# A two-layer hybrid block on one Trainium2 core: the order of its instructions set by the framework's timeline simulator instead of its simpler model

## The chip, the core and the metric

The kernel runs on one core of a Trainium2 chip. A core has a matrix engine (TensorE, PE in the rows; its weight loads are PEld), a vector engine (DVE), a scalar engine (ACT), GpSimd (POOL) and SyncE (SP), which issues the transfers here. Each engine works through its own list of instructions in the order in which it was written, and waits on semaphores where an instruction needs what another engine makes. The metric is the device time of one execution in microseconds.

## The reference, cut to what matters

Two layers work on 256 latent tokens and 256 context tokens of width 1024. The last layer needs the latent tokens alone behind its first FFN (in its mixers the context is read only).

```python
for l in range(2):
    mod = silu(c) @ ada_w[l] + ada_b[l]        # nine vectors: shift, scale, gate, three times
    x  = x + 0.5 * g1 * swiglu(modulate(rms_norm(x), sh1, sc1))          # FFN, 2816 wide
    u  = modulate(rms_norm(x), sh2, sc2)
    o_a = attention(u)     # MLA, 8 heads
    o_b = gla(u)           # gated linear attention, 4 heads, both directions, chunks of 64
    o_c = attention(u)     # GQA, 8 heads
    o_d = hyena(u)         # two long convolutions by DFT
    y   = sum(sigmoid(gate_i(u)) * (o_i @ w_branch[i]) for i in 4) @ w_out
    x  = x + g2 * y
    x  = x + 0.5 * g3 * swiglu(modulate(rms_norm(x), sh3, sc3))
```

## The kernel before

Everything is float32. A product is made of three matmuls on split operands: each operand is cut into a rounded part and the rest (`two`, L309: ACT writes `wh` at L311, DVE writes `wl` at L312, in one stage of layer 1 sometimes POOL), and `mm3` (L303) issues high by high, high by low and low by high, all at L301. Weights arrive by transfers into `wr` (three buffers) and leave the split into `wh` and `wl` (eight each).

The stages run one behind another: adaLN vectors (`ada`, L413, sixteen short matmuls with the weights of a vector from memory), statistics and norm (L487 and L513, tiles `sq`, `nacc`, `st`, `rs`, `B`, then `uh` and `ul`), the FFN (`gu`, `dn`), the mixers, the merges, `wo`, the FFN again. The mixers are chains: in the gated linear attention (GLA) a head goes from `pre` (PE) over the forget gates (ACT L992 to L994, DVE L995, L996), two scans (L998, L1000), exponentials (L1009 to L1013), products (L1014 to L1016), `AT` (PE), masks (L1026, L1030), `keT`, `ke`, `U` and the states (L1051, L1053: seven small DVE steps for each direction, one behind another) to `Og` (PE), its norm (`z`, L1065 to L1071) and `obT` (PE). Attention goes from `S` (PE) over maximum, exponential, sum, reciprocal and product (L684 to L688) to `PT` and `O` (PE). Hyena goes back and forth between spectra (`Z`, `yi` on PE) and products on ACT and DVE (`Yh`, `Yl`).

`weave` (L1326) puts beside such chains, the fill, work that waits for nothing but weights: in layer 0 the projections of `prep` (`tm`, `bk`, `bq`) beside hyena, then the merge of one finished branch (`gate`, `br`, `mt`, `y`) beside each next mixer; in layer 1 `prep` beside both attentions, and two merges beside hyena and GLA together:

```python
for c in list(chains):
    with self.first():                  # tc.high_priority(offset=200)
        if next(c, 0) is not None:
            chains.remove(c)
more = next(fill, 0) is None
```

The order on each engine isn't the order of the code. The framework takes the whole program, with priorities from the place in the code, raised by 200 in the chains (`first`) and by 400 in `evac` (L296), and hands out the instructions of each engine one by one: at each step the one that its model of time holds to be ready, the higher priority first. The model therefore decides how much fill stands between two links of a chain. Before, that is the framework's simpler model.

## Time and profile before

| | |
|---|---|
| median of three runs | 2607.05 us (2606.05 to 2609.52) |
| the profiled execution | 2601.85 us, span 2600.1 us |
| granted clock of PE, mean | 0.986 of full |
| busy: PE, DVE, ACT, POOL | 2497.5, 1696.6, 1091.1, 264.9 us |

PE is the engine that bounds; the rest of this document asks where it stands still and for whom. The rows further down tell a stretch of the span by its start and end in microseconds. A matmul's own duration overlaps that of its neighbours, so the time of dense work is read from the length of a stretch over its count.

### The profile page before, as it was taken

The page shows a single profiled execution, that of the slowest core. Times are in us where ns is not written, and L with a number is a line of the kernel's source. Part 1 is how long each engine was busy: PE and PEld are TensorE (multiplying, and loading weights), DVE is VectorE, ACT ScalarE, POOL GpSimd, SP SyncE. Part 2 cuts the span into 40 slices and gives each one's busy share as a digit, 9 for nine tenths or more (in the row PEclk, how much of TensorE's full clock was granted, in tenths as well). Part 3 has the DMA queues.
Part 4 walks back from the last instruction along what each step waited for, and adds up shares of the span by engine and source line. Part 5 has one row for each costly group of instructions (what it writes and reads, how often), then busy time and mean ns, then how long its engine had stood idle before and what let it go on. Part 6 is the DMA issues. An engine that isn't in the chain of part 4 may idle for free. (4 is left out here: it accounts for less than half of the span.)

```text
span 2600.1 us, 36866 instructions
## 1 busy us (share of the span) xinstructions
PE 2497.5 (96%) x13624; PEld 2058.8 (79%) x13624; DVE 1696.6 (65%) x3377; ACT 1091.1 (42%) x2127; POOL 264.9 (10%) x240
## 2 busy tenths in 40 slices
PE   6999999999999999999999999999999987899998
PEld 4778887887877667777888878888888777788998
DVE  5667858577547778746744466767458667776665
ACT  4333223333545554433232343232346664455554
POOL 2110003001000000020000030000020147401000
PEclk9999999999999999999999999999999999899999
DMA  7564535332313123245623244545353333356554
GB/s 253 176 213 170 190 128 192 134 108 100 126 57 122 61 88 106 89 156 174 205 97 97 86 158 146 178 146 174 102 187 130 114 120 122 114 161 210 177 184 124
DMA packets 122371, 369.01 MB, mean 142 GB/s; under 512 B 14090, under 2 KB 19660, under 8 KB 122192
## 3 DMA queue, kind: packets, MB, share of 16 engines
q1 hardware_dynamic: 122192, 366.66, 42.8%
q8 instruction: 107, 1.75, 0.3%
q14 instruction: 72, 0.59, 0.1%
HBM read 346.16 MB, written 20.45 MB: 141 GB/s over the span
## 5 line engine op out<-in xcount | busy, mean ns | idle before, releaser
L311 ACT CAST wh<-wr 128x512 fp32r<-128x512 f32 (+1 forms) x926 | 564.0, 613 | 1070.3 <-PE gu L301 396.0
L312 DVE TENSOR_TENSOR wl<-wr,wh 128x512 fp32r<-128x512 f32 (+1 forms) x854 | 577.1, 682 | 410.1 <-ACT wh L311 399.3
L301 PE MATMUL gu<-ul,wh 128*128 128x512 f32 (+1 forms) x1408 | 514.7, 366 | 2.5 <-DVE ul L542 2.5
L301 PE MATMUL gu<-uh,wh 128*128 128x512 f32 (+1 forms) x1408 | 512.3, 366 | 2.4 <-ACT uh L536 2.3
L301 PE MATMUL gu<-uh,wl 128*128 128x512 f32 (+1 forms) x1408 | 511.5, 364 | 1.3 <-DVE wl L312 1.3
L301 PE MATMUL dn<-hh,wh 128*128 128x512 f32 (+1 forms) x1408 | 389.5, 363 | 0.0
L301 PEld LDWEIGHTS gu<-ul,wh 128*128 128x128 f32 x1408 | 265.7, 189 | 58.4 <-DVE ul L542 9.3
L301 PEld LDWEIGHTS gu<-uh,wh 128*128 128x128 f32 x1408 | 265.8, 189 | 52.0 <-ACT uh L536 7.2
L301 PEld LDWEIGHTS gu<-uh,wl 128*128 128x128 f32 x1408 | 265.6, 189 | 44.0 <-DVE wl L312 1.7
L301 PEld LDWEIGHTS dn<-hh,wh 128*128 128x128 f32 x1408 | 252.6, 188 | 41.3
L301 PE MATMUL dn<-hh,wl 128*128 128x512 f32 (+1 forms) x704 | 255.3, 363 | 0.0
L502 POOL TENSOR_TENSOR nacc<-nacc,sq 128x512 f32<-128x512 f32 (+1 forms) x39 | 46.2, 1185 | 1745.1 <-ACT sq L500 1736.7
L301 PE MATMUL gate<-uh,wh 128*128 128x256 f32 (+1 forms) x768 | 202.3, 328 | 3.3 <-DVE y L1316 3.3
L464 DVE SCALAR_TENSOR_TENSOR aj<-aw,crow 128x1024 bf16<-128x1024 f32 x160 | 193.7, 1224 | 0.0
L301 PE MATMUL gate<-uh,wl 128*128 128x512 f32 (+1 forms) x512 | 177.0, 346 | 4.3 <-POOL wl L312 2.8
L301 PEld LDWEIGHTS dn<-hh,wl 128*128 128x128 f32 x704 | 132.3, 188 | 20.4
L301 PEld LDWEIGHTS gate<-uh,wh 128*128 128x128 f32 x768 | 132.0, 195 | 15.4 <-DVE y L1316 3.5
L301 PE MATMUL tm<-wh,uh 128*128 128x256 f32 x576 | 140.3, 288 | 1.6 <-ACT uh L536 1.0
L312 POOL TENSOR_TENSOR wl<-wr,wh 128x512 fp32r<-128x512 f32 x72 | 106.4, 1489 | 239.9 <-ACT wh L311 234.1
L301 PE MATMUL tm<-wl,uh 128*128 128x256 f32 x432 | 124.1, 287 | 0.0
L301 PEld LDWEIGHTS gate<-uh,wl 128*128 128x128 f32 x512 | 99.1, 194 | 15.9 <-POOL wl L312 3.0
L642 DVE SCALAR_TENSOR_TENSOR x<-dn,gt,x 128x256 f32<-128x256 f32 x168 | 74.4, 478 | 54.6 <-PE dn L301 54.6
(408 smaller groups left out, 3975.7 us busy)
## 6 DMA issues: line engine op xcount, KB each, us to landing
wr<-in_gu SPq DMA_DIRECT2D x176, 512.0 KB, 3.5
aw<-in_adat SPq DMA_DIRECT2D x80, 512.0 KB, 3.6
wr<-in_dn SPq DMA_DIRECT2D x64, 512.0 KB, 3.6
wr<-in_w_gate SPq DMA_DIRECT2D x64, 512.0 KB, 3.5
aw<-in_ada SPq DMA_DIRECT2D x48, 512.0 KB, 4.6
wr<-in_w_tm SPq DMA_DIRECT2D x36, 512.0 KB, 3.6
wr<-in_w_br SPq DMA_DIRECT2D x32, 512.0 KB, 3.5
wr<-in_dn SPq DMA_DIRECT2D x32, 384.0 KB, 3.2
```

Source lines behind the costliest of these rows:

```text
L301: self.nc.tensor.matmul(out, l, r, start=start, stop=stop)
L311: self.nc.scalar.copy(h, src)
L312: (eng or self.nc.vector).tensor_sub(l, src, h)
L464: nc.vector.scalar_tensor_tensor(out=x, in0=w, scalar=1.0, in1=self.crow[s], op0=ALU.mult, op1=ALU.mult, accum_out=o[:, s:s + 1])
L502: (nc.vector if first and k % 2 else nc.gpsimd).tensor_add(acc[:, :n], acc[:, :n], sq[:, :n])
L642: self.nc.vector.scalar_tensor_tensor(out=self.x[m][:, c], in0=p[:, c], scalar=gt[:, m, s:s + 1], in1=self.x[m][:, c], op0=ALU.mult, op1=A ...
```

## The change

One argument is added where the framework's context is made:

```diff
-    with tile.TileContext(nc, ) as tc:
+    with tile.TileContext(nc, schedule_with_timeline_sim=True) as tc:
         emit(tc, A, out)
```

No instruction is added or taken away (one of ACT's nineteen loads of a function table stands at another place); each engine's list is put in another order. PE's list changes most: most of the rows that differ lie in the woven stages. POOL's list stays almost as it was. Three places follow, all on PE; numbers behind a name are those of the buffers, the same before and after.

**Layer 0, GLA, second to third head.** `Og_9482` is the product that ends the second head, `AT_9670` the first matmul of the third behind its forget gates, `gate` and `br` are the merge. Before:

```order
L301 MATMUL Og_9482<-STl_9412,qd_9290 64x128 x2
L301 MATMUL Og_9482<-bv_8917,ATs_9393 128x128
L301 MATMUL Og_9482<-STl_9412,qd_9290 64x128 x2
L301 MATMUL Og_9482<-bv_8919,ATs_9393 128x128
L301 MATMUL Og_9482<-STc_9413,qd_9290 64x128 x2
L301 MATMUL Og_9482<-bv_8919,ATs_9393 128x128
L301 MATMUL Og_9482<-STc_9413,qd_9290 64x128 x2
L301 MATMUL gate_9537<-uh_3745,wl_9541 128x512
L301 MATMUL gate_9537<-uh_3755,wh_9544 128x512
L301 MATMUL gate_9537<-ul_3756,wh_9544 128x512
```

After:

```order
L301 MATMUL Og_9482<-STl_9412,qd_9290 64x128 x2
L301 MATMUL Og_9482<-bv_8919,ATs_9393 128x128
L301 MATMUL Og_9482<-STc_9413,qd_9290 64x128 x2
L301 MATMUL Og_9482<-bv_8919,ATs_9393 128x128
L301 MATMUL Og_9482<-STc_9413,qd_9290 64x128 x2
L301 MATMUL AT_9670<-qd_9589,ab_9597 128x128
L301 MATMUL AT_9671<-qd_9589,ab_9597 128x128
```

What moved: before, 37 `gate` and 17 `br` matmuls stand between `Og_9482` and `AT_9670`; after, none. From `AT_9381` to `obT_9878`, the last of the head behind, 36 matmuls of fill are left after (12 `gate`, 24 `br`), and the other ones stand further ahead, beside the first head and its setup. The same holds in layer 1 for the third of the GLA heads, and for the later heads of the attentions, between whose links a few `br` stand or nothing.

**Layer 0, hyena, from the first spectra to `yi`.** `tm` and `bk` are projections of `prep`. Before:

```order
L301 MATMUL tm_5177<-wh_5331,uh_3775 128x256
L301 MATMUL tm_5177<-wl_5332,uh_3775 128x256
L301 MATMUL tm_5177<-wh_5331,ul_3776 128x256
L301 MATMUL tm_5177<-wh_5331,uh_3785 128x256
L301 MATMUL tm_5177<-wl_5332,uh_3785 128x256
L301 MATMUL tm_5177<-wh_5331,ul_3786 128x256
L301 MATMUL yi_5649<-Yh_5595,dfth_4277 128x512
L301 MATMUL tm_5178<-wh_5181,uh_3715 128x256
L301 MATMUL tm_5178<-wl_5182,uh_3715 128x256
```

After:

```order
L301 MATMUL bk_5537<-ul_3776,wh_5544 128x512
L301 MATMUL bk_5537<-uh_3775,wl_5545 128x512
L301 MATMUL bk_5537<-uh_3785,wh_5544 128x512
L301 MATMUL bk_5537<-ul_3786,wh_5544 128x512
L301 MATMUL bk_5537<-uh_3785,wl_5545 128x512
L301 MATMUL bq_5611<-uh_3715,wh_5614 128x512
L301 MATMUL bq_5611<-ul_3716,wh_5614 128x512
L301 MATMUL yi_5649<-Yh_5595,dfth_4277 128x512
L301 MATMUL bq_5611<-uh_3715,wl_5615 128x512
L301 MATMUL bq_5611<-uh_3725,wh_5614 128x512
L301 MATMUL bq_5611<-ul_3726,wh_5614 128x512
L301 MATMUL bq_5611<-uh_3725,wl_5615 128x512
```

What moved: before, the fill from the last `Z` (`Z_5528`) to `yi_5649` is 73 `tm` matmuls of 256 columns; after, 42 `tm` and 50 `bk` and `bq`, these of 512 columns. The `bk` and `bq` stood beside later work.

**The norm between layer 0's second FFN and layer 1's first.** `st` sums the squares, `B` spreads the factors, `ada_13691` is the next adaLN vector, `dn` the FFN's end, `gu` the start of the next FFN. Before:

```order
L301 MATMUL st_13561<-ones_104,nacc_13560 128x1 x4
L301 MATMUL ada_13691<-aw_13692,cs_106 32x512 x2
L301 MATMUL ada_13691<-aw_13696,cs_106 32x512 x2
L301 MATMUL ada_13691<-aw_13700,cs_106 32x512
L301 MATMUL st_13561<-ones_104,sq_13581 128x1 x4
L301 MATMUL ada_13691<-aw_13700,cs_106 32x512
L301 MATMUL ada_13691<-aw_13704,cs_106 32x512 x2
L301 MATMUL ada_13691<-aw_13708,cs_106 32x512 x2
L348 MATMUL B_13606<-ident_100,rs_13591 128x128 x4
L301 MATMUL ada_13691<-aw_13712,cs_106 32x512 x2
L301 MATMUL ada_13691<-aw_13716,cs_106 32x512 x2
L301 MATMUL gu_13746<-uh_13614,wh_13738 128x512
```

After:

```order
L301 MATMUL dn_13537<-hh_13306,wl_13534 128x512
L301 MATMUL ada_13691<-aw_13712,cs_106 32x512 x2
L301 MATMUL ada_13691<-aw_13716,cs_106 32x512 x2
L301 MATMUL ada_13691<-aw_13720,cs_106 32x512 x2
L301 MATMUL st_13561<-ones_104,nacc_13560 128x1 x4
L301 MATMUL st_13561<-ones_104,sq_13581 128x1 x4
L348 MATMUL B_13606<-ident_100,rs_13591 128x128 x4
L301 MATMUL gu_13746<-uh_13614,wh_13738 128x512
L301 MATMUL gu_13781<-uh_13614,wh_13773 128x512
```

What moved: the fourteen `ada` matmuls that stood between `st` and `gu`, and two behind the first `gu`, are gone from there; six stand ahead of `st`, and the other ten over a thousand rows further up, among the FFN's matmuls. The norm behind the first FFN of layer 1 shows the same, and at the one behind the first FFN of layer 0 all sixteen moved up.

## Rows read from the trace of the kernel before

**Rows 1.** The page: busy time and share of the span of each engine
```profile
PE 2497.5 (96%) x13624; PEld 2058.8 (79%) x13624; DVE 1696.6 (65%) x3377; ACT 1091.1 (42%) x2127; POOL 264.9 (10%) x240
```

**Rows 2.** Stretches: length, busy PE, PEld, DVE, ACT, POOL (x instructions), clock, DMA share, GB/s
```profile
1180.00:1528.00 348.00, 348.00 (x1537) 288.24 (x1536) 183.72 (x325) 108.91 (x182) 7.72 (x6) 1.00 0.39 128
...
840.00:945.00 105.00, 104.47 (x512) 71.31 (x511) 73.41 (x192) 59.22 (x158) 0.00 (x0) 1.00 0.20 62
...
992.40:1076.00 83.60, 79.63 (x442) 59.74 (x441) 66.02 (x154) 33.90 (x56) 0.00 (x0) 1.00 0.32 101
...
2178.40:2233.60 55.20, 37.65 (x237) 31.92 (x236) 45.39 (x76) 21.76 (x42) 28.81 (x17) 0.85 0.31 100
```

**Rows 3.** PE's waits by releaser: total us, times, longest us
```profile
PE st L301 <- POOL nacc L502: 14.9, 2, 14.0
...
PE AT L301 <- DVE ab L1015: 10.4, 5, 4.3
...
PE obT L348 <- DVE z L1071: 7.5, 5, 3.3
...
PE yi L301 <- ACT Yh L311: 6.5, 4, 2.7
...
PE aT L348 <- ACT ck L761: 3.5, 1, 3.5
```

**Rows 4.** Groups of PE, two of 992.4 to 1076, one of 2178.4 to 2233.6: busy, mean ns
```profile
L301 PE MATMUL gate<-ul,wh 128*128 128x512 f32 x62 | 24.7, 399 | 0.0
...
L301 PE MATMUL br<-oc,wh 128*128 128x512 f32 x24 | 7.7, 402 | 0.0
...
L301 PE MATMUL gate<-uh,wh 128*128 128x256 f32 x70 | 15.8, 321 | 3.3 <-DVE y L1316 3.3
```

**Rows 5.** Groups of DVE, then of ACT, in the same stretch
```profile
L312 DVE TENSOR_TENSOR wl<-wr,wh 128x512 fp32r<-128x512 f32 x20 | 13.6, 687 | 2.8 <-issue 2.7
...
L1316 DVE SCALAR_TENSOR_TENSOR mt<-mt,br 128x512 f32<-128x512 f32 x6 | 4.0, 677 | 1.0 <-PE br L301 1.0
...
L1319 DVE TENSOR_TENSOR y<-y,mt 128x512 f32<-128x512 f32 x5 | 3.4, 682 | 0.0
...
L311 ACT CAST wh<-wr 128x512 fp32r<-128x512 f32 x21 | 12.8, 618 | 30.7 <-PE gate L301 26.1 <-PE br L301 2.4 <-DVE STl L1053 2.1
...
L1306 ACT ACTIVATE mt<-gate 128x512 f32<-128x512 f32 x6 | 3.5, 589 | 0.0
```

**Rows 6.** Groups of DVE, then of ACT, 840 to 945
```profile
L312 DVE TENSOR_TENSOR wl<-wr,wh 128x512 fp32r<-128x512 f32 x20 | 13.7, 686 | 0.5 <-ACT wh L311 0.2
...
L1319 DVE TENSOR_TENSOR y<-y,mt 128x512 f32<-128x512 f32 x7 | 4.8, 681 | 0.0
...
L311 ACT CAST wh<-wr 128x512 fp32r<-128x512 f32 x20 | 12.5, 624 | 13.7 <-PE gate L301 10.3 <-PE br L301 3.1
```

**Rows 7.** Stretches, columns as in rows 2: woven stages, and two at half clock
```profile
465.00:685.00 220.00, 212.71 (x1316) 190.27 (x1315) 146.10 (x253) 87.54 (x164) 12.51 (x12) 0.98 0.36 120
...
615.80:619.20 3.40, 3.40 (x14) 3.21 (x15) 3.40 (x6) 1.57 (x3) 0.00 (x0) 0.50 0.42 152
...
1155.10:1161.90 6.80, 5.21 (x13) 1.92 (x15) 4.96 (x15) 3.39 (x7) 3.32 (x6) 0.50 1.00 377
...
1925.00:2110.00 185.00, 177.82 (x1237) 149.60 (x1235) 125.12 (x305) 114.86 (x283) 19.48 (x14) 0.99 0.40 130
...
2110.00:2295.00 185.00, 148.56 (x1036) 132.78 (x1035) 140.00 (x271) 84.70 (x161) 93.68 (x63) 0.91 0.37 119
```

**Rows 8.** PE in order of time at a norm: start, us, what, count
```profile
1528.69 0.95 PE L301 MATMUL st<-ones,nacc 128*128 128x1 f32 x8
...
1529.57 1.90 PE L301 MATMUL ada<-aw,cs 128*32 128x512 f32 x10
...
1531.40 1.05 PE L301 MATMUL st<-ones,sq 128*128 128x1 f32 x8
...
1536.92 0.50 PE L301 MATMUL gu<-uh,wh 128*128 128x512 f32 x1 [0.42 <-ACT uh L536]
```

## The prediction, made before the changed kernel ran

> **What bounds the kernel now.** I read the page's busy times first: PE is busy for 2497.5 of 2600.1 us, 96% [rows 1]. Whatever the order is, these matmuls are the same ones, so the change can only move the time in which PE stands, runs slower, or switches between kinds of work. How dense is dense? In the FFN 1537 matmuls of 512 columns take 348.00 us, 226 ns each, and PE never stands [rows 2]. I therefore leave the FFNs aside and look at the woven stages. There the stretches tell PE's idle time as length less busy: 220.00 − 212.71 = 7.3 us in layer 0's projections and hyena, 7.2 us in layer 1's attentions, 36.4 us in layer 1's hyena and GLA, where the mean clock is down to 0.91 besides [rows 7]; in layer 0 GQA stands for 0.5 us of 105, GLA for 4.0 of 83.6 [rows 2]. The waits name the links: `AT` for `ab`, `obT` for `z`, `yi` for `Yh`, `aT` for `ck`; the longest single one, 14.0 us for `nacc`, is the start of the program and no order of later work ends it [rows 3].
>
> So the fill hides the chains almost wholly in layer 0 and partly in layer 1. Total gain to be had outside the start: some 60 us. Total to be lost: whatever a chain needs where its fill is gone.
>
> **The change part by part.** All sums are against the profiled 2601.85 us.
>
> A. *Layer 0, GLA.* In 83.6 us PE has 3 x 62 `gate` (one row of the three stands) and 24 + 18 + 12 + 8 = 62 `br` (the first stands) [rows 4]: 248 x 0.226 = 56.0 us of fill. Its own work is then 79.6 − 56.0 = 23.6 us. The new order leaves 36 fills there, 8.1 us, so PE has 31.7 us of work. What does the chain need alone? DVE is busy for 66.0 us [rows 2], of which fill is `wl` 13.6, `mt` 4.0, `y` 3.4 [rows 5]; 45.0 are the chain's. ACT is busy for 33.9, of which `wh` 12.8 and `mt` 3.5 are fill [rows 2, 5]; 17.6 are the chain's. If the two alternate strictly, three heads take 62.6 us; if ACT's steps all lie beside DVE's, 45. In the code a head's ACT steps mostly wait for DVE's and the reverse (absolute, exp, log, then the scans, then four exponentials, then the products), but the small steps of the norm and `z` of one head stand among the gates of the next. I take 57, nearer to the upper end. PE then stands for 57 − 31.7 = 25.3 us instead of 4.0: **+21** (ends +10 and +30). The 212 fills that left cost the same 226 ns where they now stand, so nothing comes back for them.
>
> B. *Layer 1, GLA and hyena.* In the third head's stretch PE is busy for 37.65 of 55.2 us [rows 2], so it stands for 17.6 although 70 + 36 + 24 + 12 + 16 + 8 = 166 `gate` matmuls of 256 columns lie in it (the first of these groups stands in [rows 4]), some 20 us at 0.12 each (an estimate: half of 0.226). The new order has most of these ahead of `pre`, where they cost the same. The chain of two mixers on one DVE, busy for 45.4 of 55.2 us, shrinks only by the fill's share of it; if it shrinks by 12 of the 20 us, that is a loss of 8. I take +8 for it, +6 for the stretch behind it, where splits now stand ahead of the spectral steps on DVE, and −5 for the one between, which gets some 96 matmuls of cover: **+9** (ends −5 and +18, from half of the 36.4 us of the whole stage [rows 7]).
>
> C. *Attention.* In GQA's 105 us PE has 240 fills, 54.2 us, and 50.2 us of its own; DVE's own is 73.4 − 13.7 − 4.8 for `y` and as much for `mt` = 50.1, ACT's 59.2 − 12.5 and 3.5 for its `mt` as in GLA = 43.2 [rows 2, 5, 6]. Four groups of heads: 12.5 us each for PE or DVE, 23.3 if DVE and ACT alternate strictly. Two heads are in flight, so I stay near the low end, 15.2. Six groups (three of GQA, two of MLA, about one in layer 1) are without fill in the new order: 6 x 2.7 = **+16** (ends 0 and +32, half the way to 23.3).
>
> D. *What the early fill gains.* Layer 0's hyena: `yi` waits for 6.5 us [rows 3], and in two stretches like the one at 615.80 (14 matmuls in 3.40 us at half clock [rows 7]) half of 6.8 us is lost. The new order has 42 x 0.12 + 50 x 0.226 = 16.3 us of cover ahead of `yi`, where 73 x 0.12 = 8.8 stood: **−10** (ends −16 and −2). Layer 1: `aT` waits for 3.5 us and gets more `tm` ahead, −4.5 with the clock that falls there; in the first half of the hyena and GLA stage some 12 of the 36.4 us go: **−16.5** (ends −25 and −4). Start and switches: fewer changes between kinds of matmul and four `gu` groups side by side at the first FFN, **−8** (ends −14 and 0).
>
> E. *The norms.* At 1529 the fourteen `ada` matmuls between `st` and `gu` cost nothing, since `st`, `rs` and `uh` come from DVE and ACT: 8.2 us from `st` to `gu`, whose end is a wait for `uh` [rows 8]. Ten matmuls take 3.8 us in the row's pitch (five in 1.90, as each shows as two). Three norms give up 16, 10 and 10 of them to dense work, 36 x 0.38 = 13.7 us; some 2 of that were in dense work before, and each gap shrinks by 0.9 us, as `st` no longer queues behind `ada`: **+8** (ends 0 and +16).
>
> At 1155 there is a norm with little beside it: PE is busy for 5.2 of 6.8 us and the granted clock is 0.50, the 1.2 GHz level [rows 7]. The norms of E would look like that. The Trainium skill, "TensorE: Matmul & The Clock Gate", section "HAM oscillation", says that gaps put the array back to half rate, so that the work behind them starts slow; the row agrees. By that rule E and A to C would each cost more, which is the third rival's case.
>
> Sum: 21 + 9 + 16 − 10 − 16.5 − 8 + 8 = +19.5, so 2621.4 for such an execution. The profiled execution lies 5.2 us below the median of 2607.05; on the median's scale I forecast **2626.5**. With the terms' ends taken as independent, the forecast's own range is 2602 to 2651.
>
> **The rivals.**
>
> 1. *Faster: the early fill is worth more than the tails cost.* The mechanism is in A and C: if a GLA head without fill takes 15 us instead of 19, because ACT's gates of the next head run fully beside DVE's states, A falls to 45 − 31.7 − 4 = +9; attention near its low end gives C = +4, B = 0, E = +5. Then 18 − 34.5 = −16.5, so **2590.5**. It decides from the point where A, B, C and E together cost less than D's 34.5 us. For it: 45 us of DVE work is the chain's own floor, and two engines side by side is what the row of GQA shows with fill. Against it: DVE waits on ACT in GLA also where PE stands idle, as 55.2 − 45.4 us in layer 1 show [rows 2].
>
> 2. *No change.* Gain and loss meet, or the orders differ in ways that PE's queue of ready work evens out: the FFNs, most of the span, are the same to a row of 226 ns. **2607**. Against it: the first two places differ by tens of matmuls, more than a wait's length. That the argument does nothing at all is excluded by the same listings.
>
> 3. *Slower by more: the clock.* In the last 185 us stage the mean clock is 0.91 with 36.4 us of idle time [rows 7]: 9 in 100 of PE's clocks, an estimate of 185 x 0.09 x 2 = 33 us at half rate. If the new tails of A, C and E, together 45 us idle, bring as much half clock each, and half of the work in it is on the chain, another 45 x 0.9 x 0.5 = 20 us and more come, with A at its upper end +9: **2655**. Against it: in a tail PE isn't what is late, so slow matmuls hide there; the fill that follows is what pays.
>
> **How the numbers follow.** Forecast 0.58, faster 0.18, no change 0.10, the clock 0.14. A measurement of this kernel can tell about 0.2% from no change, 5.2 us: below 2601.8 is faster, above 2612.3 slower. The forecast's range reaches a little into "within" (0.03 of its 0.58). So faster 0.18, same 0.13, slower 0.69. The range of 8 in 10 takes the forecast's ends and half of rivals 1 and 3: **2592 to 2656**.
>
> **What would show it.** In the profile of the changed kernel: A, in layer 0 the time from the first `AT` of the second head to the last `obT` about 57 us with some 25 us of idle time on PE, put down to `ab`, `z` and `STl`; if it is under 46, rival 1 holds. B and C, idle time before `PT` or `O` and before the third head's `AT` in layer 1. D, no wait of `yi` for `Yh` in layer 0 and no half clock there. E, no `ada` between `st` and `gu`, and idle time of 5 us and more in each of three norms; a half clock behind them speaks for rival 3. What would make the forecast wrong: FFN stretches that aren't at 226 ns any more, because weights or splits come in another order, or chains that get shorter themselves once DVE and ACT don't serve the fill between their steps.

## The result, and the profile after

The changed kernel takes **2670.65 us** (2667.83 to 2671.37, four runs) against 2608.28 of the kernel before, measured beside it: ratio 1.0235 [1.0217, 1.0252], a loss of 62.4 us. The profiled execution takes 2671.37 us, span 2669.6. I had forecast 2626.5, in a range that ended at 2656: the sign was right, the loss three times as large.

The page first: busy time and share of each engine (answers [rows 1]), and from its slices the granted clock of PE in tenths.

```profile
PE 2502.1 (94%) x13624; PEld 2078.6 (78%) x13624; DVE 1689.3 (63%) x3377; ACT 1093.4 (41%) x2127; POOL 252.2 (9%) x240
...
PEclk9999999999999998799999999999999988889999
```

The busy time of PE is 4.6 us longer and the span 69.5, so 64.9 us of it are time in which PE stands. The two dents of the clock lie in layer 0's GLA and in layer 1's mixers. Before, the same row has one slice at 8, in layer 1's mixers:

```profile
PEclk9999999999999999999999999999999999899999
```

PE's waits by releaser: total, times, longest (answers [rows 3]).

```profile
PE AT L301 <- issue: 33.7, 3, 12.5
PE ada L301 <- DMA aw<-in_ada: 18.1, 5, 12.3
PE Og L301 <- DVE STl L1053: 12.3, 3, 4.2
PE PT L348 <- DVE P L688: 10.8, 18, 1.8
PE obT L348 <- DVE z L1071: 9.8, 3, 3.8
...
PE yi L301 <- ACT Yh L311: 6.8, 1, 6.8
```

`AT` is the row that grew (before, 10.4 us for `ab` in five waits, the longest 4.3 [rows 3]): three heads, two of layer 0 and one of layer 1, wait 10.6 to 12.5 us each. The view names "issue", but the product `ab` (DVE, L1015) ends just ahead of it, as the order of time below shows. The 12.3 us for `aw` is the start of the program; before, the longest wait there was 14.0 us for `nacc` [rows 3]. The one wait of `yi`, 6.8 us, lies in layer 1; in layer 0 it no longer waits for `Yh`.

Stretches, columns as in [rows 2]: layer 0's GLA, the same from the second head's first `AT` to the last `obT`, layer 0's hyena, and four pieces of layer 1's attentions.

```profile
992.40:1076.00 83.60, 63.33 (x357) 48.25 (x358) 56.70 (x130) 28.67 (x48) 0.00 (x0) 0.87 0.27 82
...
1034.40:1108.90 74.50, 37.05 (x229) 26.10 (x228) 48.03 (x126) 19.77 (x31) 0.00 (x0) 0.68 0.17 50
...
465.00:685.00 220.00, 218.37 (x1372) 197.56 (x1371) 146.88 (x257) 89.37 (x168) 12.66 (x12) 1.00 0.38 128
...
2030.00:2050.00 20.00, 20.00 (x164) 19.65 (x163) 13.73 (x30) 13.65 (x34) 0.00 (x0) 1.00 0.60 194
2050.00:2070.00 20.00, 20.00 (x152) 17.70 (x152) 11.10 (x19) 12.87 (x26) 9.23 (x8) 1.00 0.49 145
...
2090.00:2110.00 20.00, 13.56 (x65) 7.63 (x64) 12.32 (x30) 12.14 (x33) 1.26 (x1) 0.89 0.08 27
...
2150.00:2170.00 20.00, 15.31 (x78) 9.44 (x77) 12.77 (x25) 14.33 (x33) 1.28 (x1) 0.91 0.20 66
```

In GLA PE is busy for 37 of 74.5 us, at a mean clock of 0.68. In hyena it stands for 1.6 us instead of 7.3, at full clock [rows 7]. Layer 1's attentions run dense up to about 2070 us and thin out after that, while the DMA share falls to 0.08: the fill has been spent.

One head of GLA in order of time: start, us, engine, what; in brackets the idle time ahead of it.

```profile
1046.57 0.44 PE L301 MATMUL Og<-STl,qd 128*64 128x128 f32 x4 [4.12 <-DVE STl L1053]
...
1050.55 0.60 ACT L1065 ACTIVATE z<-Og 128x512 f32<-128x512 f32 x1 [10.80 <-PE Og L301]
1051.04 0.68 ACT L992 ACTIVATE ab<-pre,vec 128x512 f32<-128x512 f32 x1
...
1052.40 1.28 ACT L994 ACT_TABLE_LOAD   x1
...
1052.96 0.16 DVE L361 TENSOR_TENSOR rs_a<-rs_y 128x4 f32<-128x4 f32 x1
...
1054.36 0.69 DVE L996 TENSOR_TENSOR la<-la,ab 128x512 f32<-128x512 f32 x1 [1.23 <-ACT ab L994]
...
1056.38 1.28 ACT L1009 ACT_TABLE_LOAD   x1 [2.05 <-DVE ab L998]
...
1059.10 0.63 ACT L1010 ACTIVATE la<-la 128x512 f32<-128x512 f32 x1 [0.34 <-DVE la L1008]
...
1060.34 0.69 DVE L1015 TENSOR_TENSOR ab<-kd,ab 128x512 f32<-128x512 f32 x1
1060.95 1.12 DVE L1071 SCALAR_TENSOR_TENSOR z<-Og,l_rs,sg 128x128 f32<-128x128 f32 x4
...
1061.13 2.08 PE L301 MATMUL AT<-qd,ab 64*128 64x128 f32 x16 [10.63 <-issue]
...
1073.20 0.70 PE L301 MATMUL Og<-STl,qd 128*64 128x128 f32 x4 [4.16 <-DVE STl L1053]
```

ACT stands 10.80 us for `Og`, then PE 10.63 us for `ab`, then PE again for the states. The links alternate over three engines. They overlap only in part: of the 26.6 us from one `Og` to the next, one of PE, DVE and ACT works alone for 15.3 us, and two or three at once for 10.7 (worked out from the trace's starts and durations).

To place the loss I took, for each pair of neighbouring matmuls of PE's trace, the time between their starts beyond the usual time of such a pair, and summed it by stage. This "lost time" holds idle time and lower clock alike; its total, 206.5 us before and 280.3 after, exceeds the difference of the spans by 4. The entries depend on what is taken as usual and where a stage is cut. By other such rules hyena's difference comes to −13 to −17, GLA's to +40 to +44, that of MLA and GQA to +13 to +18, of layer 1's attentions to +13 to +19, of its hyena and GLA to +8 to +12 and of the end to +1 to +6, so the small entries say little.

| stage | before | after | | my term |
|---|---|---|---|---|
| start, first FFN, first norm | 37.5 | 33.5 | −4.0 | D, −8 |
| L0 hyena up to MLA's first `S` | 23.6 | 7.0 | −16.6 | D, −10 |
| L0 MLA and GQA | 20.9 | 38.6 | +17.7 | C, 5 groups: +13.5 |
| L0 GLA, third merge | 16.0 | 55.7 | +39.7 | A, +21 |
| rest of layer 0, FFN, norms up to layer 1's mixers | 19.3 | 23.2 | +3.9 | E, with the end |
| L1 attentions | 23.0 | 42.3 | +19.3 | C 2.7, D −4.5 |
| L1 hyena and GLA, three stretches | 54.5 | 62.9 | +8.4 | B +9, D −12 |
| `wo`, norm, last FFN | 11.4 | 17.2 | +5.8 | E, +8 in all |

### The profile page after: what moved, and what is told of

Its sections match the earlier page's. It is cut to its first block, busy times and chain, and to the rows that moved or that the text cites. A ratio compares the mean times of both kernels' runs of the same rounds, so it can differ in the third digit from the quotient of the medians.

```text
span 2669.6 us, 36950 instructions
## 1 busy us (share of the span) xinstructions
PE 2502.1 (94%) x13624; PEld 2078.6 (78%) x13624; DVE 1689.3 (63%) x3377; ACT 1093.4 (41%) x2127; POOL 252.2 (9%) x240
## 4 chain that ended last, share of the span: by engine, by line
PE 87%; DVE 6%; ACT 3%; issue 2%; DMA 2%; SPq 0%; POOL 0%; DVEq 0%; ACTq 0%; POOLq 0%
PE gu L301 32%; PE dn L301 16%; PE gate L301 11%; PE tm L301 6%; PE dp L301 3%; PE br L301 3%; PE wo L301 2%; PE O L301 2%; PE ada L301 2%; PE S L301 1%; PE PT L348 1%; DMA aw<-in_ada 1%; PE bk L301 1%; PE Og L301 1%; ACT P L686 1%
## 5 line engine op out<-in xcount | busy, mean ns | idle before, releaser
L312 DVE TENSOR_TENSOR wl<-wr,wh 128x512 fp32r<-128x512 f32 (+1 forms) x854 | 588.1, 692 | 463.0 <-ACT wh L311 442.2
L312 POOL TENSOR_TENSOR wl<-wr,wh 128x512 fp32r<-128x512 f32 x72 | 94.7, 1324 | 266.8 <-ACT wh L311 264.3
```

The lines of the kernel that those rows point to most:

```text
L312: (eng or self.nc.vector).tensor_sub(l, src, h)
```

## The experiments

Each kernel but the paced ones is one of the two with a table of instruction numbers. For a named block of the program the table holds the instructions of the block, on each engine, in the other kernel's order; everything else stays the scheduler's choice, made anew beside what is held, so it needn't stand as in either kernel. The links cost no wait, as the time of e9 below shows (the comments are added here):

```diff
         emit(tc, A, out)
+        pin(tc, nc)   # for each neighbour in the table:
+                      # tc.add_manual_dep(ins[at], ins[prev].name, NoSync)
```

### Which blocks hold the loss

e9 is the changed kernel with all mixers of layer 0 as one block, and all of layer 1 as another, in the order of before; e10 and e11 are the kernel before with one of these blocks from the changed one.

> The changed kernel, but all of layer 0's mixers with their merges as one block, and all of layer 1's as another, keep the order of before among their own instructions, so that the places where one mixer ends and the next begins are those of before too. What stays of the change: the start and the first FFN, norms, the other FFNs, the last projection. Theory (the loss of the run with five separate weaves, 2625, sat at the places between the weaves): 6.2 us gained at the start, some 6 lost at norms and FFNs, about 2608 us, within 0.2% of before. Rival (the norms and FFNs do cost): 2625 again.

> The kernel before, but layer 0's mixers and merges as one block have the order of the changed kernel. Theory: by stretches hyena gains 16.6 us, MLA loses 4.1, GQA 13.5, GLA 36, the merge behind it 3.5: about 2607 + 40 = 2647 us.

> The kernel before, but layer 1's mixers and merges as one block have the order of the changed kernel. Theory: by stretches the attentions lose 19.3 us, hyena and GLA gain 4, lose 6.4, 6.0 and 2.9: about 2607 + 31 = 2638 us. This and the two runs ahead of it are to add up to the whole: 2671.

Measured: 2608.39 (ratio 1.0003 [0.9988, 1.0018]), 2653.78 (1.0174 [1.0146, 1.0202]) and 2626.89 (1.0069 [1.0043, 1.0095]), against 2606.86 of before. The mixers are the whole loss: +46.9 from layer 0 and +20.0 from layer 1, while start, FFNs and norms together change +1.5, which isn't clear of noise. The three sum to 68.4, 6 more than the 62.4 of the whole, so they nearly add. My terms, grouped the same way, were 21 + 13.5 − 10 = +24.5, 9 + 2.7 − 16.5 = −4.8 and 0. I was 22 us short in layer 0 and 25 in layer 1.

### Which weaves

e4 is the kernel before with layer 0's hyena weave from the changed one, e5 with all from the start to that weave.

> The kernel before, but layer 0's hyena weave with its projections has, among its own instructions, the order of the changed kernel. Theory (this is the change's gain): PE lost 16.6 us less there, so about 2608 - 16.6 = 2591.5 us, faster than before. My own size of the term was 10: 2598. Rival (the gain is borrowed from later stages, which lose it for want of the fill): within 0.2% of 2608.

> The kernel before, but everything up to and with layer 0's hyena weave (start, first FFN, its norm, hyena with its projections) has among its own instructions the order of the changed kernel. Theory: the hyena order alone gave 14.6 us; PE's lost time up to the first norm is 25.7 us before and 19.5 after, so another 6 us come, about 2586 us. Rival (the start is bound by transfers, its order is neutral): 2593, as with hyena alone.

2592.92 (0.9948 [0.9928, 0.9968]) and **2591.19** (0.9944 [0.9928, 0.996]). The hyena gain is real and stays when the later weaves keep their order: lost time there falls from 23.6 to 6.4, and the GLA behind it keeps its 10.1. It hadn't been borrowed from them. e5 is faster than both kernels, but its interval overlaps that of e4: the start, from which I had expected another 6 us, gives nothing that these runs can tell.

Then the reverse, single weaves of the changed kernel put back: e1 the GLA of layer 0 with the merge behind it, e2 the attentions of both layers, e3 layer 1's hyena and GLA, e8 as e2 with hyena held to the changed order, e6 all five weaves, each alone, with the changed order of start and hyena kept.

> The changed kernel, but the instructions of layer 0's GLA weave and of the merge behind it keep, among themselves and on every engine, the order that they had before the change. Theory (unfilled chain): the stretch from the second head's first AT to the last obT lost 38 us to idle time that nothing elsewhere gives back, so about 2670.6 - 38 = 2633 us. Rival (the loss only moves): the fill was spent earlier, where it now hides other waits; taking it from there opens those again, so no less than 2660 us. Rival (clock): if the half clock in the tail, and not the missing fill, costs the time, part of it stays behind with the other tails and the result is the same 2633, but the stretch's idle time on PE would already be small in the changed kernel, which its trace doesn't show.

> The changed kernel, but the weaves of layer 0's MLA, layer 0's GQA and layer 1's two attentions keep, each among its own instructions, the order of before. Theory (unfilled chains): 4 + 13.5 + 19.3 us of PE's lost time lie there more than before, so about 2670.6 - 37 = 2634 us. Rival (my own size of the term): 16 us, so 2654. Rival (the loss only moves): no less than 2660.

> The changed kernel, but layer 1's hyena and GLA stage with its merges keeps the order of before among its own instructions. Theory: by stretches this stage lost 6.4 + 6.0 + 2.9 us and gained 4, so about 2670.6 - 11 = 2659 us. Rival (the loss only moves): 2670. Rival (the stage is shorter with the changed order, and its losses are handed down from the attention ahead of it): slower than 2671.

> As the run in which the attentions had the order of before, but layer 0's hyena weave is held to the changed kernel's order, which that run had lost (PE lost 22.5 us there instead of 7.0). Theory: that slip hid the attentions' share, so 2664.2 - 15.5 = about 2649 us. Rival (attention's loss only moves, whatever hyena does): no less than 2660.

> The changed kernel, with the order of before in the five weaves of MLA, GQA, GLA (with the merge behind it), layer 1's attentions and layer 1's hyena and GLA; start, hyena, FFNs, norms and the end keep the changed order. It differs from the run before it in this list only in the FFNs, norms and the last projections. Theory (ada taken out of the norms costs): by stretches 0.5 + 3.1 + 1.6 - 0.8 + 3 = some 6 us more than that kernel, about 2592 us. Rival (my term of 8 us): 2594. Rival (the norms are neutral, all of the loss is in the weaves): 2586.

2638.07 (1.0119 [1.0092, 1.0147]), 2664.19 (1.022 [1.02, 1.0239]), 2664.0 (1.0219 [1.0196, 1.0242]), 2664.41 (1.0223 [1.0206, 1.024]) and 2625.18 (1.0071 [1.0053, 1.0088]). e1 gives back half of the whole loss, as term A's mechanism wants: lost time in GLA 48.2 to 10.2, though 9 of it come back in GQA and 5 in MLA, whose fill now goes earlier. e2, e3 and e8, of which I had expected 37, 11 and 22 us, give back some 6 by the medians, with intervals that overlap that of the changed kernel. e2 cures GQA, 22.9 to 11.0, and loses it where hyena hands over to MLA, 7.0 to 22.5. e8 shows that this isn't hyena's own order, since with that held the stage still has 21.6. And e6, 33 us above what I had expected, has PE's waits at such seams:

```profile
PE aT L348 <- ACT ck L761: 7.6, 2, 5.5
...
PE kT L348 <- DVE kr L879: 4.9, 1, 4.9
...
PE zT L348 <- DVE oa L312: 3.7, 1, 3.7
```

`aT` is where MLA starts, `kT` where GQA starts, `zT` where layer 1's second weave starts. The three longest add up to 14.1 us, so they don't make up the 33. Before, work of the next mixer was begun inside the weave ahead; a weave put back alone can't do that, and a table by stages blames the wrong stage.

### The clock in the tail

e7 keeps the changed order of layer 0's GLA and puts 3 x 15 and 2 x 32 matmuls, whose results nobody reads, into PE's waits: 24.6 us of more work.

```diff
+            if nq == 4 and h > 1:
+                with self.tc.issue_after(self.og):
+                    self.extra(32, X[0], wg[:, h * P:h * P + P], lr)
...
+            if nq == 4 and h > 0:
+                self.extra(15, O, wg[:, h * P:h * P + P], lr)
```

> The changed kernel, its order kept in layer 0's GLA weave, with 3 x 15 and 2 x 32 matmuls more on PE that nobody reads (24.6 us at 226 ns), put where PE stands: 15 between U and Og of the second to fourth head, 32 between Og and the AT of the next. They need no work of DVE or ACT. Theory (half clock lengthens the chain): Og at full clock takes 2.8 us instead of 4.7, AT 1.2 instead of 2.1, U less too, some 3.5 us a head, so about 2670.6 - 10 = 2660 us with the clock at 1.00 in the stretch. Rival (DVE and ACT alone set the chain): within 0.2% of 2670. Rival (the added matmuls are in the way): slower than 2676.

2663.31 (1.0217 [1.02, 1.0234]): with more work it isn't slower than the changed kernel, but 5 us faster by the ratios, whose intervals overlap, and 7 by the medians, whose runs don't (2657.73 to 2665.6 here). The stretch itself tells more. PE in order of time in e7:

```profile
1060.06 1.16 PE L301 MATMUL AT<-qd,ab 64*128 64x128 f32 x16 [3.11 <-DVE ab L1015]
...
1084.16 1.16 PE L301 MATMUL AT<-qd,ab 64*128 64x128 f32 x16 [3.08 <-DVE ab L1015]
...
1100.40 1.16 PE L348 MATMUL obT<-ident,z 128*128 128x128 f32 x4 [3.75 <-DVE z L1077]
```

The stretch of these heads in e7, columns as in [rows 2], and the third head's `AT` in the changed kernel:

```profile
1034.40:1100.90 66.50, 54.18 (x337) 40.56 (x336) 47.85 (x126) 19.68 (x31) 0.00 (x0) 0.99 0.19 56
```

```profile
1061.10:1063.20 2.10, 2.06 (x17) 1.87 (x17) 1.57 (x5) 0.00 (x0) 0.00 (x0) 0.50 0.28 44
```

`AT` takes 1.16 us instead of 2.08, and the mean clock of the execution is 0.978 instead of 0.966. From the second head's `AT` (1034.44) to the last `obT` it takes 66.0 us; in the changed kernel 1034.36 to 1108.17, 73.8. So the chain needs 66 us with PE near full clock, and the lower clock adds 8. (The 66 is an upper end, as the added matmuls can hold up a link, and this execution, 2657.73, is the fastest of the four.) The part between heads in which PE has no link, from the start of the last `Og` row to `AT`, stays: 11.3 us in the changed kernel, 11.0 here.

### Is it the early fill alone?

If all the harm lay in fill spent too soon, fill that is held back by hand should cure it. e12 issues each piece of the merge in layer 0's GLA only behind a link of the chain, e13 does so in three weaves of layer 0, e14 in layer 1 too.

```diff
+            if not pace or not chains:
+                more = next(fill, 0) is None
+            elif i % pace:
+                last = next(x for x in reversed(self.nc.cur_bb.bb.instructions) if x.engine == mybir.EngineType.PE)
+                with self.tc.issue_after(last):
+                    more = next(fill, 0) is None
```

> The changed kernel without any table: in layer 0's GLA weave a piece of the merge (24 gate and 12 br matmuls) may stand on PE only behind the chain's link after which it is traced, behind pre and behind U of each of four heads; all else is the simulator's choice. Theory (the fill was spent before the tail, pacing it gives the tail back): as with the order of before in this weave, 2670.6 - 33 = about 2638 us. Rival (the simulator's order of DVE and ACT in the tail is slow by itself): no less than 2655.

> As the run that paced the merge in layer 0's GLA alone, but the weaves of layer 0's MLA and GQA are paced too: seven of eight pieces of their merges stand behind every second link of MLA's chain, and two of every three of GQA's. Theory (a stage short of fill draws on the next one's, so that pacing the last alone only hands the shortage up): with all three paced, layer 0 loses less in each, about 2670.6 - 35 = 2636 us; the pieces are large (36 matmuls), so not all of the 47 us that layer 0's mixers cost comes back. Rival (pacing never pays, the order of DVE and ACT is what costs): no less than 2660.

> As the run ahead of it, and in layer 1's two weaves each piece of fill stands behind the chains' link after which it is traced. Theory: of the 20 us that layer 1's mixers cost about half comes back: some 10 us less than that run, about 2626 us. Rival (layer 1's chains lack fill altogether, wherever it stands): the same as that run.

2669.89 (1.0239 [1.0203, 1.0274]), 2670.28 (1.0239 [1.0223, 1.0254]) and 2685.49 (1.0296 [1.0279, 1.0314]): no gain, the last a loss. In e12 GLA's lost time falls, 48.2 to 23.3 (some 51 to 34 by another of those rules), and MLA's and GQA's grows from 38.6 to 62.3. In e13 the seam after hyena and MLA lose 48.8 us together, against 22.7 in the changed kernel. My three expectations were wrong, and with them the idea that the place of the fill on PE is the whole story. The pieces are large, 36 matmuls in e12; a finer pacing wasn't run.

### Which engine's list

So the engines were taken apart. In both mixer blocks e15 holds PE alone to the order of before, e16 all but PE, e17 PE and DVE, e18 PE and ACT; the rest is the simulator's.

> The changed kernel, but in the mixers of layer 0 and of layer 1 PE alone keeps the order of before; DVE, ACT, SP and POOL stay in the order that the simulator gives them. With all engines held this made 2608 us. Theory (where the fill stands on PE decides): about 2612 us, a few us for the other engines. Rival (the order of DVE and ACT inside the chains costs most of it): no less than 2640 us.

> The reverse of the run ahead of it: in the mixers DVE, ACT, SP and POOL keep the order of before, and PE alone is ordered by the simulator. Theory (PE's order decides): most of the loss stays, no less than 2640 us, unless the held order of the splits forces the fill to stand where it stood. Rival (DVE and ACT decide): about 2612 us.

> The changed kernel; in both mixer blocks PE and DVE are held to the order of before, ACT, SP and POOL are ordered by the simulator. Theory (PE's fill stands in front of links that DVE delivers, so PE and DVE have to agree, and the place of DVE's norm steps before z is the main disagreement): the 35.9 us for which obT waited for z with PE alone held go, no obT waits longer than 3 us, and the time falls from 2667 by at least 30, to 2615 to 2637. Rival (every engine's list has to agree; ACT's list, with the two parts wh and mt of the fill, is as much a partner as DVE's): the waits come back at links that ACT delivers, yi for Yh and gate for mt, and the time stays at 2645 or more.

> The changed kernel; in both mixer blocks PE and ACT are held to the order of before, DVE, SP and POOL are ordered by the simulator. Theory (PE and DVE have to agree): obT waits for z as with PE alone, more than 25 us in total, and the time is 2650 or more. Rival (ACT is the partner that matters): z comes in time, since the exponentials of the next head no longer stand between, and the time is 2640 or less.

| held to the order of before | us | ratio |
|---|---|---|
| nothing (the changed kernel) | 2670.65 | 1.0235 [1.0217, 1.0252] |
| PE (e15) | 2666.74 | 1.0233 [1.0199, 1.0266] |
| DVE, ACT, SP, POOL (e16) | 2764.91 | 1.0608 [1.0567, 1.0648] |
| PE, ACT (e18) | 2653.19 | 1.0173 [1.0152, 1.0194] |
| PE, DVE (e17) | 2620.74 | 1.0051 [1.0032, 1.0069] |
| all (e9) | 2608.39 | 1.0003 [0.9988, 1.0018] |

PE's order of before, alone, gains nothing clear of noise. The row of PE's waits for `z`, in e15:

```profile
PE obT L348 <- DVE z L1071: 35.9, 7, 8.2
```

The same row in e18, with ACT held as well:

```profile
PE obT L348 <- DVE z L1071: 30.7, 7, 6.4
```

And in e17, with DVE held as well (the longest is 3.3 us, where I had said 3):

```profile
PE obT L348 <- DVE z L1071: 9.7, 5, 3.3
```

The place is the end of a GLA head. In the kernel before, ACT, DVE and PE in order of time:

```profile
1009.47 0.60 ACT L1065 ACTIVATE z<-Og 128x512 f32<-128x512 f32 x1 [2.44 <-PE Og L301]
...
1011.93 0.16 DVE L358 TENSOR_SCALAR rs_v<-l_ss 128x4 f32<-128x4 f32 x1
...
1013.72 1.13 DVE L1071 SCALAR_TENSOR_TENSOR z<-Og,l_rs,sg 128x128 f32<-128x128 f32 x4
...
1014.21 0.30 PE L348 MATMUL obT<-ident,z 128*128 128x128 f32 x1 [0.26 <-DVE z L1071]
```

And in e15, the same PE order with the simulator's DVE:

```profile
1031.94 0.60 ACT L1065 ACTIVATE z<-Og 128x512 f32<-128x512 f32 x1 [3.07 <-PE Og L301]
...
1034.40 0.16 DVE L358 TENSOR_SCALAR rs_v<-l_ss 128x4 f32<-128x4 f32 x1
...
1035.76 0.69 DVE L996 TENSOR_TENSOR la<-la,ab 128x512 f32<-128x512 f32 x1 [0.99 <-ACT ab L994]
1036.37 0.15 DVE L361 TENSOR_TENSOR rs_a<-rs_y 128x4 f32<-128x4 f32 x1
...
1037.04 1.21 DVE L998 TENSOR_TENSOR_SCAN ab<-scan,la 64x512 f32<-64x512 f32 x1
1038.18 0.13 DVE L362 TENSOR_TENSOR rs_a<-rs_a,rs_v 128x4 f32<-128x4 f32 x1
1038.33 1.22 DVE L1000 TENSOR_TENSOR_SCAN ab<-scan,la 64x512 f32<-64x512 f32 x1
...
1042.95 1.12 DVE L1071 SCALAR_TENSOR_TENSOR z<-Og,l_rs,sg 128x128 f32<-128x128 f32 x4
...
1043.45 0.45 PE L348 MATMUL obT<-ident,z 128*128 128x128 f32 x1 [7.02 <-DVE z L1071]
```

Before, DVE does the ten small steps of the finished head's norm at one go, and `z` starts 4.3 us after ACT's `z`. The simulator's list puts them between the scans and products of the next head, so it starts 11.0 us after. PE's list of before has `obT` early, some 20 matmuls behind `Og`, and more fill behind it, which stands with it. These waits are 28 us more than before (7.5 [rows 3]), about half of e15's loss. The changed PE order has no such wait, as it puts `AT` ahead of `obT`; it has no fill there either. With PE and DVE both of before the lost time in GLA is 10.1 again (e17), with PE and ACT it is 24.3 (e18; up to 32 by the other rules). The lists of ACT, SP and POOL together are worth the last 12 us, 2620.74 to 2608.39.

e16 is worse than any other. Its largest row of waits is at fill, which PE takes before the old lists of ACT and DVE have delivered for it. PE's waits:

```profile
PE gate L301 <- ACT mt L1306: 24.7, 8, 5.8
...
PE gate L301 <- DVE wl L312: 14.1, 4, 5.5
```

A list that isn't held is not the changed kernel's. In e15 DVE has `L361` behind `L996`; in the head of the changed kernel above it stands ahead of it. So these four runs pair lists of before with lists that the simulator made beside them, and don't cross the two kernels. They show that an order of before is good or bad with its partners: PE's gains nothing without DVE's, and those of DVE, ACT, SP and POOL without PE's make the changed kernel 94 us slower. No run held DVE alone or ACT alone, so what the simulator's DVE list costs beside its own PE list stays open.

Why the simulator picks these orders, no run here can tell: its durations for each engine, its rule among ready instructions, or both. That stays open.

## Why the prediction was right or wrong

**The bound** was right: PE's work is the same, and the loss is all waits and clock. The FFNs hold: from 1210 to 1558 there are 1538 matmuls in 348.00 us at full clock, where before it were 1537 [rows 2]. Here is that stretch, and the norm behind layer 0:

```profile
1210.00:1558.00 348.00, 347.37 (x1538) 283.17 (x1537) 182.86 (x325) 106.23 (x179) 4.16 (x4) 1.00 0.40 133
...
1570.30:1578.50 8.20, 4.39 (x25) 3.70 (x24) 4.65 (x15) 2.46 (x5) 2.39 (x4) 0.68 0.65 256
```

The same norm before:

```profile
1528.70:1536.90 8.20, 7.79 (x49) 3.27 (x47) 4.83 (x16) 2.38 (x5) 1.06 (x2) 1.00 0.63 236
```

**A, right in kind, too small.** The stretch took 73.8 us, not 57. The step that failed is "If the two alternate strictly, three heads take 62.6 us; if ACT's steps all lie beside DVE's, 45", with 57 taken between: it left out that PE is the third engine in that chain. PE's own 23.6 us were counted as work that fills the stretch, not as links that others wait for; with them strict alternation is 45 + 17.6 + 23.6 = 86. Near full clock the chain took 66 (e7), more than the 62.6 of DVE and ACT one behind another, so links of PE must count; they make 9 us of the miss and the lower clock 8. How far each pair of engines overlaps in it, no run separates. The third rival had that mechanism, but its 20 us were spread over all tails; and what spoke against it ("slow matmuls hide there") is refuted: `AT` and `Og` are on the chain, and slow there.

The row for it: after 10.63 us without work `AT` takes 2.08 us, at a granted clock of 0.50, the 1.2 GHz level; with work in that gap, 1.16. The Trainium skill, "TensorE: Matmul & The Clock Gate", section "HAM oscillation", says that PE falls back to half rate while it waits for a transfer, so that what follows starts cold. The waits here are for DVE and ACT, and these traces show the same of them.

**B and C in layer 1, wrong in size.** Layer 1 was to gain 4.8 us and loses 20.0. In lost time the third head's stretch is +6.4 (I had +8) and the one behind it +6.0 (+6). The failed step is C's count, "about one in layer 1" of the groups without fill: `prep` is spent by about 2070, and the attentions run nearly bare up to 2170, +19.3 in the table. e2 and e8 bear it out: with the attentions' order of before, the lost time in layer 1's attentions falls by some 9 us and in the stage behind them by 7 to 10. Their times hide it, since the seam behind layer 0's hyena takes most of that back. The gain of the first half of hyena and GLA came to 4.0 instead of 12.

**C in layer 0** was +17.7 against +13.5, near in size. The 2.7 us a group was a choice near the low end of 0 to 5.4, so that is partly luck.

**D, hyena: right and better**, −16.6 by the trace and −14.6 in e4 against −10; the clock there is full. D's start gave −4.0 of 8 by the trace, and nothing clear of noise in e5 against e4 (−1.7).

**E, right in kind; its size isn't shown.** By its own figures the term was 13.7 − 2 − 2.7 (3 x 0.9) = 9, not 8. At the norm behind layer 0 `ada` is gone from between `st` and `gu`; PE is busy for 4.39 of 8.2 us (7.79 before), at a clock of 0.68, and the seven matmuls behind take 3.0 us instead of 1.6 (7 x 0.226). PE stands for 3.8 us there, where I had 5 and more. I overlooked that the norm behind layer 0's mixers goes the other way: 16 rows of `ada` instead of 4 stand between its `st` and `gu`, at a clock of 0.81 instead of 0.71. E, the start and the rest outside the mixers come to +1.5 in e9, not told from nothing.

**The rivals.** The first, that GLA alone is quick, fell with 24 us a head at full clock. The second, no change, fell with e10 and e11. The third, with 2655, came nearest and fell short too. A rival that I didn't have is the one that e15 to e18 point to: that an order is a match between the lists of several engines. In the prediction I told the order by PE's list alone, with DVE's and ACT's counted as busy time.

## What to carry to other kernels

Price a chain that will lose its cover by all of its links in a row, on every engine, PE's at the lower clock, and not by the busy time of the two busiest engines beside it. An order is a property of all the engines' lists together: moving back one engine's list (e15, e16), or one stage without its seams (e2), can cost as much as it gains, so whole blocks are tried. Here the simulator's order is worth having for one block, layer 0's hyena, with the simpler model's for the rest: 2592.92 us, or 2591.19 with the start.

## What the runs showed of the hardware

More work can cost less than nothing: 24.6 us of matmuls that nobody reads, put into PE's waits, made a stretch 7.8 us shorter and the whole 5 to 7 us, as `Og` behind them took 2.8 us instead of 4.7. And the scalar engine loads a function table twice a head, 1.28 us each. The first load stands on the bare chain: DVE waits 1.23 us for the step behind it. The second lies beside DVE's work, as ACT itself then waits 0.34 us for DVE. In the trace of the changed kernel the next instruction starts 0.02 us behind the load (1052.40 + 1.28 to 1053.70).
